# A decoder trunk on one core: x blocks on ScalarE's queue, a first weight copy on VectorE, nine warming products

## Chip, cores and metric

The kernel runs on one core of one Trainium2 chip. Its engines are TensorE (PE; its weight loads are shown apart as PEld), VectorE (DVE), ScalarE (ACT), GpSimd (POOL) and SyncE (SP), which here only issues DMAs. The metric is the device time of one execution in microseconds; less is better.

## The reference, cut to what matters

Four pre-norm residual layers over one sequence of 256 tokens and 1024 features, all in float32. Layers 0 and 3 use differential attention, layer 1 block attention, layer 2 sliding-window attention with sinks; each is followed by a squared-ReLU MLP.

```python
h = x                                    # (1, 256, 1024)
for i in range(4):
    a = rms_norm(h, attn_norm_g[i])
    h = h + mixer_i(a)                   # qkv = a @ w_in; rotary; softmax; @ v; @ w_out
    h = h + sqrelu_mlp(rms_norm(h, mlp_norm_g[i]), mlp_w_up[i], mlp_w_down[i])
return rms_norm(h, final_norm_g)

def diff_attention(...):                 # layer 0, where the change lies
    q, k, v = split(h @ w_in)            # 1024 x 3072
    q, k = rope(q) / 8, rope(k)          # first quarter of each head's 64 features
    p = softmax(q1 k1) - lam * softmax(q2 k2)   # causal, per head
    o = rms_norm(p @ v, sub_g) * (1 - lambda_init)
    return o @ w_out
```

## The kernel before

The residual stream is held transposed: features on the 128 partitions, tokens along the columns, in four tiles hT (two blocks of 128 features x 256 tokens each). Weights stream from memory in pieces of 128 x 2048 float32 (1 MB), numbered in order of use; `fetch` issues the DMA of a piece into a tile `raw` (four buffers), always on SP's queue.

A product of two float32 matrices is made of three faster ones. `stage` splits each weight piece into a high part `whi`, rounded to the format that TensorE reads at full speed (ScalarE, L176), and a low part `wlo`, the rest (VectorE, L177). `norm_part` splits a block of the normed input in the same way into the two parts of `hg` (ScalarE L330, VectorE L331), with the gain of the norm folded in. Products are hg-high x whi, hg-low x whi and hg-high x wlo. whi and wlo have three buffers each (LOOK + 1), so the high part of a piece can be written only when TensorE has read that of three pieces before for the last time. The factor of the norm is found beside the products and applied when they leave PSUM: `norm_sum` squares hT on ScalarE (`sq`, L335) and adds up on VectorE (`acc`, L340 and L344); the products `p_sum` with a matrix of ones sum over the partitions, and GpSimd makes the factor `nr`.

The first two pieces are the start of the kernel. They come in quarters of 256 KB, each followed on SP's queue by one of the eight blocks of x (128 KB), and `stage` works on them quarter by quarter, each with its block. `proj` with `ahead` takes a step of six products (`p_in`) for each block of 128 features as soon as both have come. The next two pieces come in halves. Before the first real product TensorE multiplies a tile of ones by itself WARM = 12 times (`p_warm`).

Beside that VectorE works out the angles of the rotary embedding (`rotary_tables`, tiles an, an_lo, turns) and ScalarE their sine and cosine (`sn`, `cc`), for which it loads another function table. When the first projection has left PSUM as `qk` (L695), `rope` turns it with ropea and ropeb (L406 to L411), TensorE transposes it (`p_qk`), and the parts go to `qhl` and `kpad` for the scores `p_s`, whose exponentials are transposed (`p_t`) and multiplied by v (`p_av`); the outcome `o` (L509) is transposed again (`p_o`).

The order on each engine is set by a scheduler when the program is built; the engines then run in that order and wait for semaphores. DMAs use eight semaphores in turn, so a ninth transfer is issued only when the first has landed. The kernel can add a constraint of order alone: `behind(tc, late, ahead)`. The table TURNS names pairs of TensorE instructions, by layer, tile and number, of which the first is put behind the second.

Of the kernel before, what the change touches and what calls it, by code (L numbers as in the profile page):

```python
# [14 lines left out]
AF = mybir.ActivationFunctionType  # L15
OP = mybir.AluOpType
# [4 lines left out]
S = 256  # L21
# [6 lines left out]
NEG = -1.0e38  # L28
LOOK = 2
FAR = 5  # L30
WARM = 12
RAW = 4


# [17 lines left out]
        (("p_s", 4), ("p_in", 116)),  # L52
        (("p_s", 42), ("p_d", 38)),
        (("p_d", 150), ("p_d", 161)),
    ),
    1: (
        (("p_sum", 0), ("p_in", 31)),
# [45 lines left out]
def f(ap):  # L103
    return ap.bitcast(F32)
# [24 lines left out]
def behind(tc, late, ahead):  # L129

    tc.add_manual_dep(late, ahead.name, mybir.DependencyInfo(mybir.DependencyClass.NoSync, mybir.DependencyReason.DATA),
                      reason="behind")
# [3 lines left out]
def trunk(ctx: ExitStack, tc: tile.TileContext, xT, gains, lams, swa_row, fng, weights, out):  # L136
    nc = tc.nc
    V, A, G, T = nc.vector, nc.scalar, nc.gpsimd, Numbered(nc.tensor)
# [6 lines left out]
    def bank(tag, name):  # L145
        return ps.tile([P, 512], F32, tag=tag, name=name, bufs=4)

    def room(j, shape, name, dt=F32):

        return sb.tile(shape, dt, tag=f"slot{j}", name=name, bufs=1)  # L150
# [4 lines left out]
    def fetch(parts=1, along=None):  # L155

        i = len(fetched)
        raw = sb.tile([P, 2048], F32, tag="raw", name=f"raw{i}", bufs=RAW)
        w = 2048 // parts
        for h in range(parts):  # L160
            s = slice(h * w, (h + 1) * w)
            nc.sync.dma_start(raw[:, s], weights[i, :, s])
            if along:
                along()
        fetched.append(raw)

    def stage(w=1024, first=None):
        i = len(staged)
        raw = fetched[i]
        hi = sb.tile([P, 2048], F32R, tag="whi", name=f"whi{i}", bufs=LOOK + 1)  # L170
        lo = sb.tile([P, 2048], F32R, tag="wlo", name=f"wlo{i}", bufs=LOOK + 1)
        for h in range(2048 // w):
            if first:
                first()
            s = slice(h * w, (h + 1) * w)
            high = A.activation(hi[:, s], raw[:, s], AF.Copy)  # L176
            V.tensor_tensor(lo[:, s], raw[:, s], f(hi[:, s]), op=OP.subtract)  # L177
        highs.append(high.ins)
        staged.append((hi, lo))

    used = [0]

    def take():
        i = used[0]
        used[0] += 1
        while len(fetched) < min(weights.shape[0], i + FAR + 1):
            fetch()
        while len(staged) < min(weights.shape[0], i + LOOK + 1):
            stage()
        return staged[i]  # L190
# [5 lines left out]
    hT = [cst.tile([P, 512], F32, name=f"hT{j}") for j in range(4)]  # L196
    xv = xT.rearrange("(b p) t -> p b t", p=P)
    gn = cst.tile([P, 2 * DEPTH * 8 + 2 + NT], F32, name="gn")
    gv = gn[:, :2 * DEPTH * 8].rearrange("p (k l b) -> p k l b", k=2, l=DEPTH)
    sg = gn[:, 2 * DEPTH * 8:2 * DEPTH * 8 + 2]  # L200
    posi = gn[:, 2 * DEPTH * 8 + 2:].bitcast(I32)
    loaded = []

    def load_x():
        d = len(loaded)
        nc.sync.dma_start(hT[d // 2][:, S * (d % 2):S * (d % 2) + S], xv[:, d, :])
        loaded.append(d)

    first_act = cst.tile([P, 1], F32, name="first_act")
    V.memset(first_act, 0.0)  # L210
    A.activation(first_act, first_act, AF.Copy)
    nc.sync.dma_start(gn, gains)
    fetch(4, load_x)
    fetch(4, load_x)
    fetch(2)
    fetch(2)

# [12 lines left out]
    warm = bank("wk", "p_warm")  # L230
    for _ in range(WARM):
        T.matmul(warm[:, :P], ones, ones, start=True, stop=True)
# [10 lines left out]
    def bcast(dram, n):  # L243
        return bass.AP(tensor=dram.tensor, offset=dram.offset, ap=[[0, P], [1, n]])
# [6 lines left out]
    def rotary_tables():  # L251

        posf = cst.tile([P, NT], F32, name="posf")
        V.tensor_copy(posf, posi)
        an = cst.tile([P, NT, 8], F32, name="an")
        lo = cst.tile([P, NT, 8], F32, name="an_lo")
        V.tensor_tensor(an, invt, posf[:, :, None].to_broadcast([P, NT, 8]), op=OP.mult)
        G.memset(lo, 0.0)

        for turn, bits in ((2.0 ** 16 * math.pi, 10), (2.0 * math.pi, 9), (2.0 * math.pi, 20)):  # L260
            q = cst.tile([P, NT, 8], F32, name="turns")
            V.tensor_scalar(q, an, 1.0 / turn, None, op0=OP.mult)
            V.tensor_scalar(q, q, 12582912.0, None, op0=OP.add)
            V.tensor_scalar(q, q, -12582912.0, None, op0=OP.add)
            for x in (an, an, lo):
                m, e = math.frexp(turn)
                c = math.ldexp(math.floor(m * 2 ** bits), e - bits)
                turn -= c
                V.scalar_tensor_tensor(x, q, -c, x, op0=OP.mult, op1=OP.add)
            if bits == 10:  # L270
                yield
            V.scalar_tensor_tensor(lo, q, -turn, lo, op0=OP.mult, op1=OP.add)
            if bits != 20:
                V.tensor_tensor(q, an, lo, op=OP.add)
                V.tensor_tensor(an, an, q, op=OP.subtract)
                V.tensor_tensor(lo, an, lo, op=OP.add)
                V.tensor_copy(an, q)
        V.tensor_tensor(an, an, lo, op=OP.add)
        pi = 3.1415925
        V.tensor_scalar(an, an, pi, -pi, op0=OP.min, op1=OP.max)  # L280
        ab = cst.tile([P, NT, 8], F32, name="ab")
        V.scalar_tensor_tensor(ab, an, -1.0, an, op0=OP.mult, op1=OP.max)
        V.tensor_scalar(ab, ab, -1.0, math.pi / 2, op0=OP.mult, op1=OP.add)
        A.activation(sn, an, AF.Sin)
        A.activation(cc[:, :, 0:8], ab, AF.Sin)
        V.tensor_copy(cc[:, :, 8:16], cc[:, :, 0:8])
        V.tensor_scalar(nsn, sn, -1.0, None, op0=OP.mult)

    def lambdas():
        lam_init = [0.8 - 0.6 * math.exp(-0.3 * i) for i in (0, 3)]  # L290
        lv = room(4, [P, 4, 2, HD], "lv")
        nc.sync.dma_start(lv, bcast(lams, 8 * HD))
        lp = sb.tile([P, 2, 2, HD], F32, tag="ropea", name="lp")
        V.tensor_tensor(lp, lv[:, 0::2], lv[:, 1::2], op=OP.mult)
        ls = cst.tile([P, 2, 2], F32, name="ls")
        V.tensor_reduce(ls, lp, axis=AX.X, op=OP.add)
        A.activation(ls, ls, AF.Exp)
        V.tensor_tensor(nlam, ls[:, 1], ls[:, 0], op=OP.subtract)
        for s in range(2):
            V.tensor_scalar(nlam[:, s:s + 1], nlam[:, s:s + 1], -lam_init[s], None, op0=OP.add)  # L300
            V.tensor_scalar(sg[:, s:s + 1], sg[:, s:s + 1], 1.0 - lam_init[s], None, op0=OP.mult)

    def rsqrt(y, x, n, by_power=False):

# [19 lines left out]
    def norm_part(n, d):  # L324

        j, b = d // 2, d % 2
        if b == 0:
            n.both.append(sb.tile([P, 2, 2, S], F32R, tag=f"hg{j}", name=f"hg{j}", bufs=1))
        both, h, g = n.both[j][:, b], hT[j][:, S * b:S * b + S], n.gain[:, d:d + 1]
        A.activation(both[:, 0], h, AF.Copy, scale=g)  # L330
        V.scalar_tensor_tensor(both[:, 1], h, g, f(both[:, 0]), op0=OP.mult, op1=OP.subtract)  # L331

    def norm_sum(n, j):
        sq = sb.tile([P, 512], F32, tag="relu", name="sq")
# [251 lines left out]
    def mixer_layer(i, n):  # L586
# [46 lines left out]
        else:  # L633
# [36 lines left out]
            def LAM(_):  # L670
                if i == 0:
                    lambdas()
# [53 lines left out]
    def into(n, d, p, row, whole=False):  # L726

        j, b = d // 2, d % 2
        h = hT[j][:, S * b:S * b + S]
        y = p  # L730
        if not whole:
            y = sb.tile([P, S], F32, tag="y", name="y")
            joined(y, p)
        if row is not None:
            V.tensor_tensor(y, y, row, op=OP.mult)
        V.tensor_tensor(h, y, h, op=OP.add)  # L736
        norm_part(n, d)
        if b:
            norm_sum(n, j)
# [78 lines left out]
    def down_out(us, res, factor):  # L818
# [35 lines left out]
        for c in range(2):  # L854
# [29 lines left out]
            else:  # L884
# [10 lines left out]
                finish(1, 2)  # L895

    tables = rotary_tables()
    next(tables)
    n = new_norm(gv[:, 0, 0, :])
    blocks = iter(range(8))  # L900
    for _ in range(2):
        stage(512, lambda: norm_part(n, next(blocks)))
# [114 lines left out]
```

## Time and profile before

| | |
|---|---|
| Median of 3 runs | 1141.01 us (1140.76 to 1141.21) |
| Profiled execution | 1140.76 us; its span is 1139.0 us |
| TensorE busy | 1130.0 us, 99% of the span |
| VectorE, ScalarE busy | 825.5 us (72%), 660.7 us (58%) |
| Read from memory | 196.52 MB, 173 GB/s over the span |
| Mean granted clock of TensorE | 0.999 |

The span goes from the first instruction of the program to the last; the time of an execution has a little more around it. A row of the timeline has start and duration in us, engine (a q behind it stands for the queue that issues DMAs), line, operation, output and inputs by the program's names, sizes, a count where equal rows were merged, and in brackets how long the engine had been idle and what released it. A name without its number stands for all buffers of that name.

### The profile page before, as it was taken

How to read it: one execution, taken by the hardware profiler on the slowest of the kernel's cores; microseconds unless marked ns; L12 is line 12 of the kernel's file. 1: busy time of each engine (PE TensorE's matmuls, PEld its weight loads, DVE VectorE, ACT ScalarE, POOL GpSimd, SP SyncE). 2: the span in 40 equal slices, each digit the busy share in tenths (PEclk: the TensorE clock that was granted, in tenths of full speed). 3: DMA queues.
4: the chain of work that ended last, by engine and by line, in shares of the span. 5: the costliest groups of instructions: out<-in, count | busy, mean ns of one | idle time of the engine just before them, and what ended most of it. 6: DMA issues, size and time to landing. Idle time of an engine off the chain costs nothing.

```text
span 1139.0 us, 17026 instructions
## 1 busy us (share of the span) xinstructions
PE 1130.0 (99%) x6560; PEld 986.0 (87%) x6560; DVE 825.5 (72%) x1584; ACT 660.7 (58%) x1207; POOL 13.2 (1%) x43
## 2 busy tenths in 40 slices
PE   9999999999999999999999999999999999999997
PEld 8889988888888888888899998888888899888886
DVE  8878977656676698766569887765667788777453
ACT  7866656544476665654446765554446766665342
POOL 2000000000000000000000000000000000000000
PEclk9999999999999999999999999999999999999999
DMA  8543555555544355555553346555554435554551
GB/s 330 197 148 118 175 197 196 196 193 185 185 148 148 116 181 190 197 201 189 185 209 112 111 152 218 185 187 191 190 200 138 145 134 164 197 195 167 185 185 37
DMA packets 30608, 198.66 MB, mean 174 GB/s; under 512 B 3520, under 2 KB 5184, under 8 KB 7360
## 3 DMA queue, kind: packets, MB, share of 16 engines
q1 hardware_dynamic: 30240, 197.06, 50.2%
q8 instruction: 51, 0.84, 0.3%
q10 hardware_dynamic: 288, 0.52, 0.1%
q14 instruction: 29, 0.24, 0.1%
HBM read 196.52 MB, written 1.05 MB: 173 GB/s over the span
## 4 chain that ended last, share of the span: by engine, by line
PE 94%; DVE 3%; issue 1%; ACT 1%; DMA 0%; SPq 0%; POOLq 0%; POOL 0%; DVEq 0%; ACTq 0%
PE p_up L118 31%; PE p_down L118 23%; PE p_in L118 17%; PE p_last L118 7%; PE p_d L118 6%; PE p_s L118 3%; PE p_av L118 2%; PE p_t L121 1%; DVE wlo L177 1%; PE p_qk L121 1%; PE p_e L118 1%; DMA raw<-in_weights 0%; PE p_o L121 0%; ACT junk L504 0%; ACT whi L176 0%
## 5 line engine op out<-in xcount | busy, mean ns | idle before, releaser
L177 DVE TENSOR_TENSOR wlo<-raw,whi 128x1024 fp32r<-128x1024 f32 (+1 forms) x374 | 446.5, 1209 | 201.3 <-ACT whi L176 200.8
L176 ACT ACTIVATE whi<-raw 128x1024 fp32r<-128x1024 f32 (+1 forms) x374 | 383.8, 1046 | 207.8 <-issue 110.5
L118 PE MATMUL p_up<-hg,whi 128*128 128x512 f32 x1024 | 356.1, 394 | 0.0
L118 PE MATMUL p_up<-hg,wlo 128*128 128x256 f32 x1024 | 283.7, 278 | 0.0
L118 PE MATMUL p_down<-uu,whi 128*128 128x512 f32 x768 | 266.4, 393 | 0.0
L118 PEld LDWEIGHTS p_up<-hg,whi 128*128 128x128 f32 x1024 | 191.7, 187 | 43.4
L118 PE MATMUL p_down<-uu,wlo 128*128 128x256 f32 x768 | 213.5, 278 | 0.0
L118 PE MATMUL p_in<-whi,hg 128*128 128x512 f32 (+1 forms) x736 | 212.7, 371 | 0.0
L118 PEld LDWEIGHTS p_up<-hg,wlo 128*128 128x128 f32 x1024 | 192.6, 188 | 0.5
L118 PEld LDWEIGHTS p_down<-uu,whi 128*128 128x128 f32 x768 | 143.9, 187 | 32.8
L118 PEld LDWEIGHTS p_in<-whi,hg 128*128 128x128 f32 x736 | 132.9, 189 | 22.4 <-ACT hg L330 0.2
L118 PEld LDWEIGHTS p_down<-uu,wlo 128*128 128x128 f32 x768 | 144.5, 188 | 0.0
L118 PE MATMUL p_in<-wlo,hg 128*128 128x512 f32 (+1 forms) x368 | 130.1, 368 | 0.0
L118 PE MATMUL p_d<-oo,whi 128*128 128x256 f32 (+1 forms) x416 | 85.0, 295 | 0.0
L803 ACT ACTIVATE uu<-u 128x512 fp32r<-128x512 f32 x64 | 40.5, 632 | 73.4 <-DVE u L801 73.4
L118 PE MATMUL p_last<-whi,uu 128*128 128x512 f32 (+1 forms) x264 | 79.4, 383 | 0.0
L118 PEld LDWEIGHTS p_in<-wlo,hg 128*128 128x128 f32 x368 | 68.8, 189 | 11.4 <-DVE wlo L177 0.5
L723 ACT ACTIVATE cross<-p_up 128x256 f32<-128x256 f32 x128 | 47.9, 374 | 37.3 <-PE p_up L118 35.3
L118 PEld LDWEIGHTS p_d<-oo,whi 128*128 128x128 f32 x416 | 66.3, 191 | 1.9 <-issue 0.2
L330 ACT ACTIVATE hg<-hT,gn 128x256 fp32r<-128x256 f32 x64 | 31.4, 503 | 60.6 <-DVE hT L736 60.6
L441 ACT ACTIVATE e<-ns,nm 128x256 f32<-128x256 f32 (+1 forms) x128 | 56.8, 446 | 13.5 <-DVE nm L438 13.3
L118 PE MATMUL p_d<-oo,wlo 128*128 128x256 f32 x224 | 63.9, 286 | 0.0
(168 smaller groups left out, 1073.4 us busy)
## 6 DMA issues: line engine op xcount, KB each, us to landing
raw<-in_weights SPq DMA_DIRECT2D x181, 1024.0 KB, 4.8
raw<-in_weights SPq DMA_DIRECT2D x8, 256.0 KB, 4.6
raw<-in_weights SPq DMA_DIRECT2D x4, 512.0 KB, 7.0
hT<-in_xT SPq DMA_DIRECT2D x8, 128.0 KB, 4.5
bias<-in_swa_row SPq DMA_DIRECT2D x1, 512.0 KB, 3.7
grow<-in_fng SPq DMA_DIRECT2D x1, 512.0 KB, 3.5
out<-res SPq DMA_DIRECT2D x4, 128.0 KB, 2.1
out<-res ACTq DMA_DIRECT2D x2, 256.0 KB, 2.2
```

The source lines that it names most:

```text
L118: return self.keep(out.tensor.name.rstrip("_0123456789"), self.engine.matmul(out, *args, **kw))
L121: return self.keep(out.tensor.name.rstrip("_0123456789"), self.engine.transpose(out, *args, **kw))
L176: high = A.activation(hi[:, s], raw[:, s], AF.Copy)
L177: V.tensor_tensor(lo[:, s], raw[:, s], f(hi[:, s]), op=OP.subtract)
L330: A.activation(both[:, 0], h, AF.Copy, scale=g)
L441: A.activation(e[:, s], ns[:, s], AF.Exp, bias=nm[:, t:t + 1], scale=-1.0, accum_out=l[:, t:t + 1])
L723: A.activation(cross, p[:, S:], AF.Copy)
L803: A.activation(both[:, :, 0], r3(2)(u), AF.Copy)
```

## The change

- Four blocks of x (0 to 3) are issued on ScalarE's queue: two ahead of its first table load and two behind `first_act`. SP issues the gains, four quarters of the first weight piece in a row, then block 4, then the second piece's four quarters with blocks 5 to 7 behind the first three.
- The high part of the first quarter of the first piece is copied by VectorE and not by ScalarE. Three constraints put that copy behind an instruction of the angles, the first low part of hg behind the copy, and the first wlo behind that.
- The two scalings of `sg` in `lambdas` are put behind the last instruction of the angles' list.
- WARM is 9 instead of 12.
- Layer 0 has twenty more pairs in TURNS.

In the order that is built from it, TensorE's instructions differ from the old order only within layer 0. There p_sum stands behind the product p_in 56, a little later than before; p_qk is preceded by seven products more of the third projection's start and the second's end; on ScalarE the load of the table for sine stands behind the first half of the sixth weight piece's whi; on VectorE the halves of the third and fourth piece's wlo follow each other with few instructions of the angles between them.

```diff
-WARM = 12
+WARM = 9
 TURNS = {
     0: (
...
+        (("p_sum", 0), ("p_in", 56)),
+        (("p_in", 98), ("p_qk", 7)),
+        (("p_in", 114), ("p_s", 6)),
+        (("p_s", 7), ("p_in", 114)),
+        (("p_in", 115), ("p_s", 11)),
+        (("p_in", 116), ("p_s", 2)),
+        (("p_in", 117), ("p_s", 5)),
+        (("p_t", 0), ("p_in", 136)),
+        (("p_qk", 8), ("p_t", 0)),
+        (("p_t", 1), ("p_qk", 9)),
+        (("p_qk", 10), ("p_t", 2)),
+        (("p_in", 137), ("p_qk", 15)),
+        (("p_s", 12), ("p_in", 158)),
+        (("p_t", 3), ("p_s", 15)),
+        (("p_in", 159), ("p_t", 5)),
+        (("p_s", 13), ("p_in", 161)),
+        (("p_in", 162), ("p_s", 17)),
+        (("p_in", 165), ("p_s", 23)),
+        (("p_t", 6), ("p_in", 173)),
+        (("p_in", 174), ("p_t", 6)),
...
             nc.sync.dma_start(raw[:, s], weights[i, :, s])
             if along:
-                along()
+                along(h)
...
         for h in range(2048 // w):
-            if first:
-                first()
+            normed = first() if first else None
             s = slice(h * w, (h + 1) * w)
-            high = A.activation(hi[:, s], raw[:, s], AF.Copy)
-            V.tensor_tensor(lo[:, s], raw[:, s], f(hi[:, s]), op=OP.subtract)
+            if i + h:
+                high = A.activation(hi[:, s], raw[:, s], AF.Copy)
+                V.tensor_tensor(lo[:, s], raw[:, s], f(hi[:, s]), op=OP.subtract)
+            else:
+                copied = V.tensor_copy(hi[:, s], raw[:, s]).ins
+                behind(tc, copied, angles[1])
+                behind(tc, normed, copied)
+                behind(tc, V.tensor_tensor(lo[:, s], raw[:, s], f(hi[:, s]), op=OP.subtract).ins, normed)
...
-    used = [0]
+    used, angles = [0], []
...
-    def load_x():
+    def load_x(queue=nc.sync):
         d = len(loaded)
-        nc.sync.dma_start(hT[d // 2][:, S * (d % 2):S * (d % 2) + S], xv[:, d, :])
+        queue.dma_start(hT[d // 2][:, S * (d % 2):S * (d % 2) + S], xv[:, d, :])
         loaded.append(d)
 
     first_act = cst.tile([P, 1], F32, name="first_act")
     V.memset(first_act, 0.0)
+    load_x(nc.scalar)
+    load_x(nc.scalar)
     A.activation(first_act, first_act, AF.Copy)
     nc.sync.dma_start(gn, gains)
-    fetch(4, load_x)
-    fetch(4, load_x)
+    load_x(nc.scalar)
+    load_x(nc.scalar)
+    fetch(4)
+    load_x()
+    fetch(4, lambda h: h < 3 and load_x())
     fetch(2)
     fetch(2)
...
-                V.scalar_tensor_tensor(x, q, -c, x, op0=OP.mult, op1=OP.add)
+                angles.append(V.scalar_tensor_tensor(x, q, -c, x, op0=OP.mult, op1=OP.add).ins)
...
-            V.tensor_scalar(sg[:, s:s + 1], sg[:, s:s + 1], 1.0 - lam_init[s], None, op0=OP.mult)
+            late = V.tensor_scalar(sg[:, s:s + 1], sg[:, s:s + 1], 1.0 - lam_init[s], None, op0=OP.mult)
+            behind(tc, late.ins, angles[-1])
...
-        V.scalar_tensor_tensor(both[:, 1], h, g, f(both[:, 0]), op0=OP.mult, op1=OP.subtract)
+        return V.scalar_tensor_tensor(both[:, 1], h, g, f(both[:, 0]), op0=OP.mult, op1=OP.subtract).ins
```

## The prediction

> **What bounds the kernel now.** I read the page first: its busy shares and the chain that ended last.
>
> ```profile
> span 1139.0 us, 17026 instructions
> PE 1130.0 (99%) x6560; PEld 986.0 (87%) x6560; DVE 825.5 (72%) x1584; ACT 660.7 (58%) x1207; POOL 13.2 (1%) x43
> PE 94%; DVE 3%; issue 1%; ACT 1%; DMA 0%; SPq 0%; POOLq 0%; POOL 0%; DVEq 0%; ACTq 0%
> ```
>
> TensorE is busy for 1130.0 of 1139.0 us, and 94% of the chain is its own. The diff touches the first 30 us, and the built order of the changed program differs from the old one in layer 0 alone, so nothing can be won beyond the waits of TensorE there. The windows of the early stretch come next (columns: stretch, its length, busy time of TensorE, weight loads, VectorE, ScalarE, GpSimd, then granted clock, DMA share, GB/s).
>
> ```profile
> 1.00:6.00 5.00, 5.00 (x23) 5.00 (x24) 2.32 (x11) 2.43 (x5) 4.72 (x22) 1.00 0.66 197
> 16.00:30.00 14.00, 13.97 (x66) 11.33 (x65) 13.45 (x43) 11.90 (x15) 0.71 (x1) 1.00 0.92 367
> ```
>
> Two things to see. From 16 to 30 us VectorE is busy for 13.45 of 14.00 us: what is inserted or moved there is late for somebody. And TensorE counts as busy from 1 us on, although until 6 us it only multiplies ones. The timeline shows what ends that, and at which rate the first real products run.
>
> ```profile
> 0.72 1.28 ACT L211 ACT_TABLE_LOAD   x1 [0.72 <-PEq L1006]
> 0.98 5.49 PE L118 MATMUL p_warm<-ones 128*128 128x128 f32 x24 [0.98 <-POOL ones L221]
> 1.17 0.42 SPq L162 DMA_DIRECT2D raw<-in_weights  x1
> 1.64 0.42 SPq L206 DMA_DIRECT2D hT<-in_xT  x1
> 4.68 0.63 ACT L176 ACTIVATE whi<-raw 128x512 fp32r<-128x512 f32 x1 [2.46 <-DMA raw<-in_weights]
> 5.22 0.49 ACT L330 ACTIVATE hg<-hT,gn 128x256 fp32r<-128x256 f32 x1
> 5.35 0.69 DVE L177 TENSOR_TENSOR wlo<-raw,whi 128x512 fp32r<-128x512 f32 x1 [0.93 <-ACT whi L176]
> 6.12 1.48 PE L118 MATMUL p_in<-whi,hg 128*128 128x512 f32 x4
> 7.90 1.09 PE L118 MATMUL p_in<-whi,hg 128*128 128x512 f32 x4
> 8.80 0.33 SPq L162 DMA_DIRECT2D raw<-in_weights  x1
> 9.29 1.08 PE L118 MATMUL p_in<-whi,hg 128*128 128x512 f32 x4
> 18.53 0.17 DVE L277 COPY an<-turns 128x16 f32<-128x16 f32 x1
> ```
>
> The operands of the first product, whi and hg, are ready at 5.22 + 0.49 = 5.71 us, but the twelve warming products last to 6.12 (0.43 us each, from 5.14 / 12). The first step of six products takes 7.90 - 6.12 = 1.78 us, the second 9.29 - 7.90 = 1.39. The excess of 0.39 us is that of 1.7 products which take 0.46 instead of 0.23 us: TensorE runs at half its rate until about 6.9 us, whatever the clock column says.
>
> **The change, part by part.** Landings first (KB, us from issue to landing, for the first weight quarter, the first block of x and the last quarter of the second piece):
>
> ```profile
> raw<-in_weights SPq DMA_DIRECT2D x1, 256.0 KB, 3.5
> hT<-in_xT SPq DMA_DIRECT2D x1, 128.0 KB, 3.4
> raw<-in_weights SPq DMA_DIRECT2D x1, 256.0 KB, 4.5
> ```
>
> *Queues.* The quarter lands at 1.17 + 3.5 = 4.67 us, the block behind it at 1.64 + 3.4 = 5.04, so 128 KB more cost 0.37 us. In the changed program SP issues the quarter at the same place, and ScalarE's queue brings two blocks of x beside it. The quarter then lands between 4.67 (nothing shared) and 5.04 (one block ahead of it); I take 4.9. The four issues cost ScalarE some 0.4 us each and push its table load and first_act back by 0.8 us; its fourth issue waits for the landing of block 0, with the first hg behind it in the queue. ScalarE has 2.46 us of idle time before its first whi to hide all that. If the cover were gone, hg would be late and the first product with it, by up to the 1.6 us of the four issues. The bytes in all are the same, so I leave the landing of the last quarter (issued at 8.80, landing at 13.3) where it is.
>
> *Copy on VectorE.* The trace has no copy of 512 columns there. It costs at least 0.17 us (16 columns) and at most 0.69 (wlo, same size, two sources); I take 0.5, nearer to the row of its size. First product: 4.9 + 0.5 = 5.4 us, between 4.9 and 5.8.
>
> *Nine warming products.* They end at 0.98 + 9 x 0.43 + 0.2 = 5.0 us, so they no longer hold the first product, and TensorE stands idle for some 0.4 us. The 0.7 us between 5.4 and 6.12 are run at half rate, so the head start is worth 0.36 us (0.15 to 0.6). In the row TensorE was busy without a break from 0.98 us and the rate doubled at 6.9. [...]
>
> *First low part of the third weights.* The rows of before, from the last quarter on:
>
> ```profile
> 13.55 0.62 ACT L176 ACTIVATE whi<-raw 128x512 fp32r<-128x512 f32 x1
> 14.47 0.62 ACT L335 ACTIVATE sq<-hT 128x512 f32<-128x512 f32 x1
> 14.76 0.69 DVE L177 TENSOR_TENSOR wlo<-raw,whi 128x512 fp32r<-128x512 f32 x1
> 15.36 0.48 DVE L331 SCALAR_TENSOR_TENSOR hg<-hT,gn,hg 128x256 fp32r<-128x256 f32 x1
> 15.76 0.68 DVE L340 TENSOR_TENSOR acc<-acc,sq 128x512 f32<-128x512 f32 x1
> 16.48 0.42 DVE L344 TENSOR_TENSOR acc<-acc 128x256 f32<-128x256 f32 x1
> 17.26 0.60 PE L118 MATMUL p_sum<-ones,acc 128*128 128x128 f32 x4
> 17.32 1.22 DVE L177 TENSOR_TENSOR wlo<-raw,whi 128x1024 fp32r<-128x1024 f32 x1
> 18.60 0.19 PEld L118 LDWEIGHTS p_in<-wlo,hg 128*128 128x128 f32 x1 [0.47 <-DVE wlo L177]
> ```
>
> Before, wlo of the last quarter ends at 15.45, and 1.87 us later (hg, one acc, the folding acc, four small ones) VectorE starts the first half of the third piece's wlo; TensorE waits for it at 18.60. In the changed order ScalarE does a square (0.62) ahead of the last quarter's whi, so that whi ends at about 13.3 + 0.6 + 0.6 = 14.5 and its wlo at 15.3, and between it and the next wlo stand two acc instead of one (+0.6), no hg (-0.4), and three small ones (-0.1): 2.0 us. The wlo starts at 17.3 and TensorE goes on at about 18.5, as before; the head start is lost in this wait, which grows. By then TensorE had also done the two products p_sum, which a new pair of TURNS puts eleven products later; they are worth about 4 x 0.11 = 0.45 us and are still to be done. So TensorE is 0.45 - 0.1 = 0.35 us behind here. If the last quarter's chain comes 0.8 us earlier, it is 0.45 ahead; if it comes 0.3 later, 0.65 behind.
>
> *Rotary tables and p_qk.*
>
> ```profile
> 23.23 1.28 ACT L284 ACT_TABLE_LOAD   x1
> 25.37 0.22 ACT L284 ACTIVATE sn<-an 128x16 f32<-128x16 f32 x1 [0.86 <-DVE an L280]
> 26.45 0.20 ACT L285 ACTIVATE cc<-ab 128x16 f32<-128x16 f32 x1
> 27.12 2.00 ACT L176 ACTIVATE whi<-raw 128x1024 fp32r<-128x1024 f32 x2
> 27.73 1.22 DVE L177 TENSOR_TENSOR wlo<-raw,whi 128x1024 fp32r<-128x1024 f32 x1
> 28.87 0.42 DVE L411 TENSOR_TENSOR qk<-ropea,ropeb 128x256 f32<-128x256 f32 x1
> 29.60 1.03 PE L121 MATMUL p_qk<-ident,qk 128*128 128x128 f32 x8
> 76.50 5.46 PE p_in L118 x24
> ```
>
> Before, ScalarE loads its Sin table at 23.23, ahead of the two halves of the sixth piece's whi (27.12). In the changed order the first of these halves stands ahead of the table load, and it waits until TensorE has read the third piece's whi for the last time, since three buffers take turns. Counted from the end of that read: half a whi 1.05, table 1.28, sn 0.22, cc 0.20, less 0.1 for each overlap, is 2.5 us; the second half of the whi ends at 3.5; on VectorE its wlo (1.22) now stands between the rotary products and the sum qk, so 4.7; qk (0.42) ends at 5.1, and p_qk can start at about 5.2. TensorE has 21 products between that read and p_qk in the changed order, 22 distances of 0.2275 us (5.46 / 24) less the 0.4 us that the read itself lasts: 4.6 us. So it waits 0.6 us, and 0.1 more for a weight load that is no longer hidden: +0.7 us (0 if the table is loaded ahead after all, 1.2 if VectorE is half a us late as well). Before, TensorE met qk without an idle row. Queued behind the waiting whi on ScalarE are the tables, the other half and the next qk; all of layer 0 waits for p_qk.
>
> *Later in layer 0.*
>
> ```profile
> 35.16 0.35 PE L118 MATMUL p_s<-kpadl,qhl 128*128 128x256 f32 x1 [0.15 <-DVE kpadl L584]
> 65.70 0.69 DVE L509 TENSOR_TENSOR o<-p_av,ry 128x512 f32<-128x512 f32 x1
> 66.94 0.60 PE L121 MATMUL p_o<-ident,o 128*128 128x128 f32 x4
> ```
>
> From p_qk to the first p_s there are as many products as before, so the small wait at 35.16 stays. Between the first p_av and p_o there are three fewer: 0.68 us of cover against 66.94 - 66.39 = 0.55 of slack, +0.1 us (0 to 0.5). The two scalings of the gains (0.4 us in all) only move, into a VectorE that is waited for; they are in the terms above.
>
> Sum: +0.35 + 0.7 + 0.1 = +1.15 us on the profiled execution (1140.76 us, its span and 1.76 around it): 1141.9. The median of the three runs is 1141.01, 0.25 above the profiled one, so I forecast a median of 1142.1 us. What a measurement of this kernel can tell from no change is about 0.2%, or 2.3 us: edges at 1138.7 and 1143.3. My forecast is a loss too small to tell.
>
> **The rivals.** *The half rate lasts longer.* [...] A quarter: 0.25.
>
> *The waits don't come and the head start stays.* VectorE and ScalarE had 0.9 and 2.5 us of idle time before their first work; if x comes early enough that both are 0.8 us ahead at the last quarter, the first term is -0.45, and if the sixth piece's whi does not hold the table, the second is 0: 1140.6 on the median's scale, and 1140.0 with the small waits gone as well. Against it speaks the order in the built program. 0.18. To be faster by over 0.2% it would also need the waits that stand in the rest of the layer to go, perhaps a third of this.
>
> *The streaming is late.* SP has at most eight transfers under way; the second piece's quarters wait for landings of the first ones, and these now share with x. If the last quarter lands 1 us later, the first low part is 1 us later: 1143.1. The row of 4.5 us for a quarter under load against 3.5 at the start speaks for it, the equal bytes against it. 0.07.
>
> **How the numbers follow.** Forecast 0.5, rivals 0.25, 0.18 and 0.07. Slower by over 0.2%: 0.18 of the first rival, 0.05 of the third, 0.05 from a forecast whose terms all end at their upper bounds (0.65 + 1.2 + 0.5 = 2.35): 0.28. Faster by over 0.2%: 0.06. Within: 0.66. The range goes from 1140.0 (second rival) to 1143.9 (first rival with half a us more), which leaves out no more than 2 in 10.
>
> **What would show it.** Right: the first p_in at about 5.4 us after a gap, the first p_in from the third piece's wlo still at 18.3 to 18.8, an idle row before p_qk of about 0.6 us with ScalarE's Sin table loaded behind a half of whi, less than 5 us ahead of p_qk. The half-rate rival shows in a second and third step of 2.7 us instead of 1.39. Wrong: no idle row at p_qk, or the low part before 17.8 us; then the second rival holds. A wait anywhere else in layer 0 over 0.5 us that I have not named would make the sum wrong even at the right time.

## The result and the profile after

The changed kernel took 1143.64 us (median of 12 runs, 1142.57 to 1144.59), the kernel before 1140.95 (12 runs, 1140.46 to 1141.74). The ratio is 1.0023, 95% interval 1.0016 to 1.0031: 2.7 us slower, 0.24%. The profiled execution of the changed kernel took 1144.19 us, 3.43 more than that of the kernel before (1140.76).

From the page of the changed kernel, busy times and the chain that ended last:

```profile
span 1142.4 us, 17013 instructions
PE 1129.5 (99%) x6554; PEld 982.6 (86%) x6554; DVE 826.2 (72%) x1585; ACT 660.1 (58%) x1206; POOL 13.2 (1%) x43
PE 96%; DMA 1%; DVE 1%; issue 1%; ACT 1%; SPq 0%; POOLq 0%; POOL 0%; DVEq 0%; ACTq 0%
```

TensorE does the same work but for the three warming products, the span is 3.4 us longer, and a DMA has 1% of the chain, where it had 0%. The windows of the early stretch (length, then busy time of TensorE, weight loads, VectorE, ScalarE, GpSimd, granted clock, DMA share, GB/s):

```profile
1.00:6.00 5.00, 4.03 (x18) 3.84 (x18) 1.93 (x8) 2.33 (x4) 4.72 (x22) 1.00 0.76 210
16.00:30.00 14.00, 12.03 (x53) 9.08 (x52) 12.40 (x35) 10.33 (x13) 0.71 (x1) 1.00 0.95 377
```

From 16 to 30 us TensorE is busy for 12.03 instead of 13.97 us, and VectorE and ScalarE, which were to be the cause of any loss, have more idle time than before. All of them wait for something from outside. The timeline shows the start, and then what is waited for:

```profile
0.98 4.05 PE L138 MATMUL p_warm<-ones 128*128 128x128 f32 x18 [0.98 <-POOL ones L252]
5.48 0.81 DVE L200 CAST whi<-raw 128x512 fp32r<-128x512 f32 x1 [1.06 <-DMA raw<-in_weights]
6.43 1.16 PE L138 MATMUL p_in<-whi,hg 128*128 128x512 f32 x4 [1.40 <-DVE whi L200]
7.98 1.21 PE L138 MATMUL p_in<-whi,hg 128*128 128x512 f32 x4
16.34 0.63 ACT L196 ACTIVATE whi<-raw 128x512 fp32r<-128x512 f32 x1 [1.94 <-DMA raw<-in_weights]
16.88 1.14 ACT L367 ACTIVATE sq<-hT 128x512 f32<-128x512 f32 x2
17.00 0.69 DVE L197 TENSOR_TENSOR wlo<-raw,whi 128x512 fp32r<-128x512 f32 x1 [1.80 <-ACT whi L196]
17.70 0.69 DVE L372 TENSOR_TENSOR acc<-acc,sq 128x512 f32<-128x512 f32 x1
18.49 0.69 DVE L372 TENSOR_TENSOR acc<-acc,sq 128x512 f32<-128x512 f32 x1
19.21 0.43 DVE L376 TENSOR_TENSOR acc<-acc 128x256 f32<-128x256 f32 x1
20.83 0.50 PE L138 MATMUL p_in<-wlo,hg 128*128 128x512 f32 x1 [0.95 <-DVE wlo L197]
22.78 0.60 PE L138 MATMUL p_sum<-ones,acc 128*128 128x128 f32 x4
```

The first product is later than before (6.43 against 6.12), not earlier. ScalarE then stands idle for 1.94 us until the last quarter of the second piece has landed; VectorE idles behind it, and the first product on the third piece's low part starts at 20.83 instead of 18.60. That is 2.23 of the 3.43 us. The landings (KB, us from issue to landing) of the first weight quarter, issued at 1.17, and of the last quarter of the second piece, issued at 9.29:

```profile
raw<-in_weights SPq DMA_DIRECT2D x1, 256.0 KB, 4.3
raw<-in_weights SPq DMA_DIRECT2D x1, 256.0 KB, 7.0
```

They land at 5.45 and 16.32; before, at 4.66 and 13.26. The last quarter is also issued later, at 9.29 and not at 8.80. SP's rows in the timeline show where the queue stands still:

```profile
3.07 0.43 SPq L232 DMA_DIRECT2D hT<-in_xT  x1
5.66 0.33 SPq L182 DMA_DIRECT2D raw<-in_weights  x1
9.29 0.43 SPq L182 DMA_DIRECT2D raw<-in_weights  x1
```

SP issues nothing from 3.50 to 5.66 us. The wait ends 0.02 us after block 1 of x, which ScalarE's queue had issued at 1.18, has landed (5.64). The row waits for the semaphore of that block: the 212 transfers of the trace have eight between them, and the blocks on ScalarE's queue take some of these.

The rest of the loss, 1.20 us, comes behind the low part, and p_qk carries most of it:

```profile
29.33 1.07 ACT L196 ACTIVATE whi<-raw 128x1024 fp32r<-128x1024 f32 x1 [0.36 <-PE p_in L138]
30.41 1.28 ACT L315 ACT_TABLE_LOAD   x1
31.93 1.05 ACT L196 ACTIVATE whi<-raw 128x1024 fp32r<-128x1024 f32 x1
33.01 1.23 DVE L197 TENSOR_TENSOR wlo<-raw,whi 128x1024 fp32r<-128x1024 f32 x1
34.16 0.42 DVE L443 TENSOR_TENSOR qk<-ropea,ropeb 128x256 f32<-128x256 f32 x1
34.72 1.06 PE L141 MATMUL p_qk<-ident,qk 128*128 128x128 f32 x8 [0.67 <-DVE qk L443]
70.32 0.42 PEld L141 LDWEIGHTS p_o<-ident,o 128*128 128x128 f32 x4 [0.30 <-ACT v L722]
```

A half of whi waits for TensorE, the Sin table stands behind it, a wlo stands ahead of qk, and TensorE waits for qk. The distance from the start of the product ahead of it to its own is 0.83 us longer than such a distance without a wait. p_o has a wait of its own (0.26 us by the same count), the first p_s of layer 0, which waited 0.33 us before, has none.

### The profile page after: what moved, and what is told of

Same layout as the page of the kernel before. It is cut to its first block, busy times and chain, and to the rows that moved or that the text cites. A ratio compares the mean times of both kernels' runs of the same rounds, so it can differ in the third digit from the quotient of the medians.

```text
span 1142.4 us, 17013 instructions
## 1 busy us (share of the span) xinstructions
PE 1129.5 (99%) x6554; PEld 982.6 (86%) x6554; DVE 826.2 (72%) x1585; ACT 660.1 (58%) x1206; POOL 13.2 (1%) x43
## 3 DMA queue, kind: packets, MB, share of 16 engines
q10 hardware_dynamic: 864, 1.05, 0.3%
HBM read 196.52 MB, written 1.05 MB: 173 GB/s over the span
## 4 chain that ended last, share of the span: by engine, by line
PE 96%; DMA 1%; DVE 1%; issue 1%; ACT 1%; SPq 0%; POOLq 0%; POOL 0%; DVEq 0%; ACTq 0%
PE p_up L138 31%; PE p_down L138 23%; PE p_in L138 18%; PE p_last L138 7%; PE p_d L138 6%; PE p_s L138 3%; PE p_av L138 2%; PE p_t L141 1%; DMA raw<-in_weights 1%; PE p_qk L141 1%; PE p_e L138 1%; DVE wlo L197 0%; PE p_o L141 0%; ACT junk L536 0%; PE p_sum L138 0%
## 5 line engine op out<-in xcount | busy, mean ns | idle before, releaser
L473 ACT ACTIVATE e<-ns,nm 128x256 f32<-128x256 f32 (+1 forms) x128 | 56.8, 446 | 13.1 <-DVE nm L470 12.9
```

The source lines that it names most:

```text
L473: A.activation(e[:, s], ns[:, s], AF.Exp, bias=nm[:, t:t + 1], scale=-1.0, accum_out=l[:, t:t + 1])
```

## The experiments

**What is held.** The order of the instructions is made by a scheduler that looks at the loads too, so a change of the loads alone would change the order as well. In all kernels below but r_same the order of computation on TensorE, VectorE and ScalarE is therefore held, by a chain of dependences that adds no semaphore, to that of the kernel before ("old order") or of the changed one ("new order"):

```diff
+    for engine, places in ORDER.items():
+        for late, ahead in zip(places[1:], places):
+            behind(tc, made[engine][late], made[engine][ahead])
```

The table has them all. Landing is that of the last quarter of the second piece: the trace has sixteen events for each transfer (3392 for 212 in the kernel before), read here as one from each of the core's sixteen DMA engines; the columns give the eighth and the last of them. "Low part" is the start of the first product on the third piece's low part. The profiled time and the low part stand with their difference to the kernel before, "rest" is the one difference less the other. Times in us.

| kernel | loads, order | landing: 8th, last | low part | profiled | rest | median (runs) |
|---|---|---|---|---|---|---|
| before | old, old | 12.32, 13.26 | 18.60 | 1140.76 | | 1140.96 (33) |
| changed | new, new | 13.21, 16.32 | 20.83 (+2.23) | 1144.19 (+3.43) | 1.20 | 1143.64 (12) |
| r_same | new, new | 13.86, 16.22 | 20.74 (+2.14) | 1144.09 (+3.33) | 1.19 | 1143.87 (6) |
| p_old_loads | old, new | 12.90, 13.54 | 20.00 (+1.40) | 1143.35 (+2.59) | 1.19 | 1142.92 (10) |
| p_new_loads | new, old | 13.08, 15.84 | 20.38 (+1.78) | 1142.49 (+1.73) | -0.05 | 1142.72 (11) |
| p_old_order | new, old | 13.38, 16.01 | 20.55 (+1.95) | 1142.78 (+2.02) | 0.07 | 1142.68 (11) |
| p_x_between | see there, new | 12.40, 12.98 | 18.96 (+0.36) | 1142.29 (+1.53) | 1.17 | 1142.85 (11) |
| p_quarters | see there, new | 13.46, 15.62 | 20.13 (+1.53) | 1143.25 (+2.49) | 0.96 | 1142.62 (11) |
| p_spacer | see there, new | 13.72, 14.75 | 19.71 (+1.11) | 1143.01 (+2.25) | 1.14 | 1142.59 (11) |
| p_tables | new, see there | 13.37, 15.84 | 20.35 (+1.75) | 1143.40 (+2.64) | 0.89 | 1143.40 (11) |
| p_swap | see there, old | 12.66, 14.58 | 19.11 (+0.51) | 1141.18 (+0.42) | -0.09 | 1141.18 (11) |
| p_copy_only | old, old | 12.67, 13.51 | 18.82 (+0.22) | 1140.98 (+0.22) | 0.00 | 1140.98 (11) |
| p_xb_old | see there, old | 12.35, 14.17 | 19.77 (+1.17) | 1141.81 (+1.05) | -0.12 | 1141.62 (11) |
| p_tuned | old, see there | 12.53, 13.21 | 19.11 (+0.51) | 1141.32 (+0.56) | 0.05 | 1141.12 (11) |

The column "rest" is the main finding: whatever the loads, the profiled time is that of the kernel before, plus the delay of the low part, plus nothing in the old order and 1.1 to 1.2 us in the new one (0.96 in p_quarters). From the first product of layer 0's MLP (`p_up`) to the end, all fourteen profiled executions take 1019.4 to 1019.8 us, so the differences arise ahead of it. The kernel before ran beside each series, with medians of 1140.95 to 1141.08. The intervals of the ratios are about 0.0009 to either side, 1 us, so the medians alone separate only the larger steps.

**r_same: was the late landing chance?**

> The changed kernel once more, unaltered, for a second profile. Theory A (the new loads make the last quarter of the second piece land late each time): it lands at 16.0 to 16.6 us again, two DMA engines behind the other fourteen by over 2 us, the first product on the third piece's low part starts at 20.5 to 21 us, and the median is 1143.6. Theory C (two DMA engines were late by chance in the one execution that was profiled): it lands by 14.5 us, the low part is taken up by 19.3 us, and the profiled execution takes 1142.8 us or less.

```profile
16.25 0.63 ACT L196 ACTIVATE whi<-raw 128x512 fp32r<-128x512 f32 x1 [1.14 <-DMA raw<-in_weights]
20.74 0.50 PE L138 MATMUL p_in<-wlo,hg 128*128 128x512 f32 x1 [1.09 <-DVE wlo L197]
```

The timeline of the second profile repeats the first: landing at 16.22, low part at 20.74, median 1143.87 (ratio 1.0027, 1.0015 to 1.0038). Theory C falls. One engine lagged this time, by 1.3 us, not two.

**Loads and order, crossed: p_old_loads, p_new_loads, p_old_order.** The first is the changed kernel with

```diff
-    load_x(nc.scalar)
-    load_x(nc.scalar)
     A.activation(first_act, first_act, AF.Copy)
     nc.sync.dma_start(gn, gains)
-    load_x(nc.scalar)
-    load_x(nc.scalar)
-    fetch(4)
-    load_x()
-    fetch(4, lambda h: h < 3 and load_x())
+    fetch(4, lambda h: load_x())
+    fetch(4, lambda h: load_x())
```

the second the kernel before with the reverse of it, the third the changed kernel, loads and all, in the old order.

> The changed kernel with the loads of the kernel before (quarters and blocks of x alternate on SP's queue), every engine's order of computation held to that of the changed kernel. Theory A (loads): the last quarter lands at 13.3 us as in the kernel before, the first product on the third piece's low part starts at 18.5 to 19.0, only the wait for p_qk (0.7 us) and what was predicted for p_sum (0.35) and p_o (0.1) remain, and the median is 1142.0 (1141.7 to 1142.4). Theory B (the new order of the engines costs it all): 1143.6 (1143.2 to 1144.0), as with the new loads.

> The kernel before with the new loads alone (four blocks of x on ScalarE's queue, the first four quarters in a row on SP's), every engine's order of computation held to that of the kernel before, twelve warming products, ScalarE making the first high part. Theory A (loads): the last quarter lands at 16 us, the first product on the third piece's low part at 20.5 instead of 18.6, the median is 1143.0 (1142.4 to 1143.6). Theory B (order): 1141.0 (1140.6 to 1141.4), whatever the landings do.

> The changed kernel (new loads, the copy on VectorE, nine warming products) with every engine's order of computation held to that of the kernel before: p_sum early, the Sin table ahead of the sixth piece's high part; the scalings of the gains stay late. Theory A (loads): within 0.3 us of the kernel before with the new loads alone, 1143.0, since a head start is lost in the wait for the low part. Theory B (order): 1141.0 or, with a head start of 0.4 us kept, 1140.6.

p_new_loads came out at 1142.72 us (ratio 1.0017, 1.0008 to 1.0026), p_old_order at 1142.68 (1.0015, 1.0006 to 1.0024): theory A, and the copy with nine warming products is worth nothing beside it. In the timeline of p_new_loads the last quarter's high part waits for its landing as in the changed kernel:

```profile
15.86 0.63 ACT L221 ACTIVATE whi<-raw 128x512 fp32r<-128x512 f32 x1 [1.60 <-DMA raw<-in_weights]
20.38 0.50 PE L221 MATMUL p_in<-wlo,hg 128*128 128x512 f32 x1 [0.24 <-DVE wlo L221]
```

p_old_loads missed both theories: 1142.92 (1.0022, 1.0013 to 1.0032). The landing was in time (13.54), the low part was not (20.00). Its timeline says why:

```profile
14.67 0.62 ACT L240 ACTIVATE sq<-hT 128x512 f32<-128x512 f32 x1
15.19 0.61 ACT L240 ACTIVATE whi<-raw 128x512 fp32r<-128x512 f32 x1
15.48 0.68 DVE L240 TENSOR_TENSOR acc<-sq 128x512 f32<-128x512 f32 x1
16.08 0.69 DVE L240 TENSOR_TENSOR wlo<-raw,whi 128x512 fp32r<-128x512 f32 x1
18.72 2.35 DVE L240 TENSOR_TENSOR wlo<-raw,whi 128x1024 fp32r<-128x1024 f32 x2
20.00 0.50 PE L240 MATMUL p_in<-wlo,hg 128*128 128x512 f32 x1 [0.91 <-DVE wlo L240]
```

In the new order a square stands ahead of the last quarter's whi on ScalarE, and an acc ahead of its wlo on VectorE. With the old loads ScalarE reaches that whi at 15.19, 1.65 us after the landing and 1.64 later than before (13.55). So both halves of the change delay the same low part by themselves, 1.78 and 1.40 us, and together by 2.23: the delays overlap.

**What delays the last quarter: p_x_between, p_quarters, p_swap, p_spacer.** In the changed kernel a block of x stands ahead of each quarter of the second piece, and the first half of the third piece directly behind the last. The four kernels: in the changed one, blocks behind the quarters again,

```diff
     fetch(4)
-    load_x()
-    fetch(4, lambda h: h < 3 and load_x())
+    fetch(4, lambda h: load_x())
```

the third piece in quarters,

```diff
-    fetch(2)
+    fetch(4)
     fetch(2)
```

a spare block between the last quarter and the third piece,

```diff
     fetch(4, lambda h: h < 3 and load_x())
+    nc.sync.dma_start(room(12, [P, 512], "spare")[:, :S], xv[:, 7, :])
```

and, in the kernel before, the last block and the last quarter exchanged (the number is that of the blocks issued behind each quarter):

```diff
-    fetch(4, load_x)
+    fetch(4, lambda h: (1, 1, 2, 0)[h])
```

> The changed kernel with one thing undone in the loads: in the second piece each block of x stands behind a quarter again (quarter, x, quarter, x ... instead of x, quarter, x, quarter ...), so that the last block, not the first half of the third piece, follows the last quarter on SP's queue. Order of computation as in the changed kernel. Theory A1 (the last quarter is late for the bytes ahead of it): one block of 128 KB less, 0.4 us, landing at 15.6 to 15.9 us, median 1143.4. Theory A2 (it is late because the transfers right behind it, with rows of 4 KB, take the bandwidth from the engines that lag): landing at 13.3 to 14.2, the third piece's low part taken up at 18.9 to 19.3, median 1142.2 (1141.9 to 1142.6).

> The changed kernel with the third piece fetched in four quarters instead of two halves, so that rows of 2 KB instead of 4 KB stand behind the last quarter of the second piece. Order of computation as in the changed kernel. Theory A1 (bytes ahead): the last quarter lands at 16.0 to 16.3 as before, median 1143.6. Theory A2 (large rows behind it): landing at 13.5 to 14.5 us, median 1142.2 to 1142.8.

> The kernel before with two neighbours in SP's queue exchanged: the last block of x is issued ahead of the last weight quarter of the second piece, not behind it, so that the first half of the third piece follows the quarter directly. Nothing else changes, and every engine's order is that of the kernel before. Theory A1 (128 KB more ahead of the quarter is what counts): landing at 13.6 to 13.9 us instead of 13.3, median 1141.1 (1140.9 to 1141.4). Theory A2 (what counts is that the half with its rows of 4 KB stands right behind it): landing at 15.4 to 16.2, the third piece's low part taken up at 20 us, median 1142.4 (1141.8 to 1143.0).

> The changed kernel with one load more: the last block of x is fetched a second time, into a buffer that nobody reads, between the last quarter of the second piece and the first half of the third. Order of computation as in the changed kernel. Theory A1 (bytes ahead): the quarter lands at 16.0 to 16.3 as in the changed kernel and the median is 1143.7 or, for 128 KB more ahead of the third piece, 1144.0. Theory A2 (what follows): landing at 13.4 to 14.2, the third piece's low part taken up at 19 to 19.5, median 1142.8 (1142.3 to 1143.1).

Rows of p_x_between, p_quarters, p_spacer and p_swap, from their timelines in this order:

```profile
14.31 0.61 ACT L240 ACTIVATE whi<-raw 128x512 fp32r<-128x512 f32 x1
18.96 0.51 PE L240 MATMUL p_in<-wlo,hg 128*128 128x512 f32 x1 [0.92 <-DVE wlo L240]
```

```profile
15.64 0.63 ACT L240 ACTIVATE whi<-raw 128x512 fp32r<-128x512 f32 x1 [0.69 <-DMA raw<-in_weights]
20.13 0.51 PE L240 MATMUL p_in<-wlo,hg 128*128 128x512 f32 x1 [0.98 <-DVE wlo L240]
```

```profile
15.04 0.62 ACT L240 ACTIVATE whi<-raw 128x512 fp32r<-128x512 f32 x1
19.71 0.50 PE L240 MATMUL p_in<-wlo,hg 128*128 128x512 f32 x1 [0.92 <-DVE wlo L240]
```

```profile
14.60 0.63 ACT L221 ACTIVATE whi<-raw 128x512 fp32r<-128x512 f32 x1 [1.01 <-DMA raw<-in_weights]
19.11 0.50 PE L221 MATMUL p_in<-wlo,hg 128*128 128x512 f32 x1 [0.23 <-DVE wlo L221]
```

Where a block stands behind the quarter (p_x_between, p_spacer), the row of the last quarter's whi waits for no DMA any more, and what stands ahead of it on ScalarE sets its start; where the third piece follows, the wait is there. Neither theory holds alone; the landings of p_quarters (15.62), p_spacer (14.75) and p_swap (14.58) lie between the two expectations. The landing has two parts. The eighth engine is through at 12.3 to 12.9 us where the last block stands behind the quarter and at 12.7 to 13.9 where it stands ahead (eight kernels, p_swap with 12.66 the lowest): that is A1, some 0.8 us between the means (12.53 and 13.34). All of it is in the issue: the quarter is issued at 8.63 us on average in the first six kernels and at 9.48 in the eight, and from the issue to the eighth engine it takes 3.90 and 3.87 us. So the place in the queue makes the issue later, and the transfer itself is not slower up to the eighth engine. The last engine trails the eighth by 1.9 to 3.1 us in the seven kernels in which the third piece follows the quarter directly, and by 0.6 to 1.8 in the seven in which a block does: that is A2, and it is the larger part. The two groups nearly touch (p_swap 1.92, p_xb_old 1.82) and only the changed kernel was profiled twice, so that the third piece behind the quarter makes the lag is likely and not shown. The size of the rows does not explain it: with rows of 2 KB behind the quarter (p_quarters) the lag was 2.16 us, of the same kind as with 4 KB. What slows the one to four late engines was not found.

In time: p_x_between 1142.85 (1.0016, 1.0007 to 1.0025), p_quarters 1142.62 (1.0012, 1.0003 to 1.0021), p_spacer 1142.59 (1.0014, 1.0005 to 1.0023), each 0.8 to 1.3 us below the changed kernel's two medians, which is at the edge of what medians separate here; in the profiled executions 1.9 us lie between p_x_between and the changed kernel. p_x_between's median is 0.25 us above what A2 allowed; p_quarters' is within A2 although its landing was nearer to A1; p_swap's with 1141.18 (1.0002, 0.9993 to 1.0011) within A1 although its landing was between the two.

**p_tables: the tables ahead again.** Up to p_sum and the first two qk as in the changed kernel, from there on the old order:

> The changed kernel up to p_sum and the first two qk; from there on every engine in the order of the kernel before, so that the Sin table is loaded ahead of the sixth piece's high part and the 17 later turns are undone. Loads new, last quarter at 16.0 to 16.3 us. As predicted for this part: the wait of 0.83 us at p_qk and that of 0.26 at p_o go, that at the first p_s (0.3 us) comes back, median 1142.9 (1142.7 to 1143.1). Rival (what waits at p_qk is late from the landing of the third piece and waits elsewhere): 1143.5 to 1143.9.

```profile
32.08 0.86 PEld L239 LDWEIGHTS p_qk<-ident,qk 128*128 128x128 f32 x8 [0.52 <-issue]
37.83 0.36 PE L239 MATMUL p_s<-kpadl,qhl 128*128 128x256 f32 x1 [0.29 <-DVE kpadl L239]
```

1143.40 (1.002, 1.0011 to 1.0029), between the two expectations. In its timeline the wait at p_qk shrinks from 0.83 to 0.28 us, that at p_o is gone, and that at p_s is back with 0.46 instead of 0.33. Worked out: p_sum behind the low part 0.45, plus 0.28, plus 0.46 - 0.33, is 0.86; the "rest" of the table is 0.89. For the changed kernel the same count is 0.45 + 0.83 + 0.26 - 0.33 - 0.11 (a later p_s that waits 0.11 instead of 0.22) = 1.10, against 1.20.

**p_copy_only: the head start alone.** The kernel before with the copy, nine warming products and the late scalings:

```diff
-WARM = 12
+WARM = 9
-            high = A.activation(hi[:, s], raw[:, s], AF.Copy)
+            copied = V.tensor_copy(hi[:, s], raw[:, s]).ins
...
```

> The kernel before with the copy on VectorE and nine warming products alone (and the scalings of the gains late), old loads, every engine's order held to that of the kernel before. First product at 5.4 to 5.6 us instead of 6.12. Theory D (a head start is lost in the wait for the third piece's low part): 1140.9 (1140.6 to 1141.2). Rival (the head start stays): 1140.4 to 1140.6.

```profile
4.54 0.60 DVE L241 CAST whi<-raw 128x512 fp32r<-128x512 f32 x1
5.50 0.75 PE L241 MATMUL p_in<-whi,hg 128*128 128x512 f32 x2 [0.31 <-ACT hg L241]
18.82 0.19 PEld L241 LDWEIGHTS p_in<-wlo,hg 128*128 128x128 f32 x1 [0.50 <-DVE wlo L241]
```

The first product comes 0.6 us earlier, the low part does not: 1140.98 us (0.9999, 0.999 to 1.0007). Theory D holds.

**p_xb_old and p_tuned: a version that beats both?** The first puts the loads of p_x_between, the copy and nine products into the old order. The second is p_copy_only with three places of VectorE's order changed.

> The loads of p_x_between (four blocks of x on ScalarE's queue, the first four quarters in a row, in the second piece each block behind its quarter), the copy on VectorE and nine warming products, with every engine's order of computation that of the kernel before. If the place of the last quarter is all that the new loads cost: landing at 13.0 us, median 1141.0 (1140.6 to 1141.3), 1.7 us less than with the loads as they were changed. If they cost something of their own (blocks of x or the other quarters late): 1141.8 to 1142.7.

> An attempt to beat both: the kernel before with the copy on VectorE and nine warming products, and three places of VectorE's order changed. The third piece's first low part goes ahead of four small instructions of the rotary tables (0.2 us of wait at 18.6 us go, and 0.3 of the head start stays), the second kpadl ahead of a low part (0.33 us of wait at the first p_s), and o ahead of a low part (0.65 us of wait at p_o, 111 us). If all three waits go: 1139.6 (1139.3 to 1140.2). Rival (each low part that is put back is waited for in its place): 1140.7 to 1141.5.

Neither does: 1141.62 (1.0005, 0.9996 to 1.0014), between its two expectations, and 1141.12 (1.0, 0.9991 to 1.0008), as the rival had it. In p_tuned the waits at p_s and at p_o are gone, but the low parts that were put back are waited for, at 21.39 us for instance. In p_xb_old the last quarter landed at 14.17 us and not at 13.0, although a block stands behind it: one engine lagged by 1.4 us, and the first row below waits for it. Its profile shows something else too, in TensorE's rows:

```profile
14.20 0.63 ACT L241 ACTIVATE whi<-raw 128x512 fp32r<-128x512 f32 x1 [0.41 <-DMA raw<-in_weights]
5.86 2.05 PE L241 MATMUL p_in<-whi,hg 128*128 128x512 f32 x4 [0.67 <-DVE whi L241]
7.71 1.05 PE L241 MATMUL p_in<-wlo,hg 128*128 128x512 f32 x2
8.56 1.82 PE L241 MATMUL p_in<-whi,hg 128*128 128x512 f32 x4
10.21 0.63 PE L241 MATMUL p_in<-wlo,hg 128*128 128x512 f32 x2
```

Two products on the low part take 1.05 us at 7.71 and 0.63 at 10.21: half rate until about 10.2 (the trace's record of full rate begins at 10.15, in the kernel before at 6.78). TensorE then never waits for the third piece's low part, which it reaches at 19.77, and the execution is 1.05 us longer than that of the kernel before. This is what the prediction's first rival names, a half rate that lasts longer, in one of the eleven profiled executions with nine warming products.

## Why the prediction was right, and where not

The time lies in the range (1143.64 in 1140.0 to 1143.9), 1.5 us above the point; the loss is just past the edge of what can be told from no change, and the prediction gave a loss of that size 0.28. That the range holds the time is in part luck: its upper end was there for the half rate, which did not come, and the late landing used that room. By the prediction's own sign, the low part at 18.3 to 18.8 us, the sum was wrong, for it came at 20.83.

*The landing of the last quarter* is the step that failed: "The bytes in all are the same, so I leave the landing of the last quarter (issued at 8.80, landing at 13.3) where it is." It landed at 15.8 to 16.3 us in all five profiles with these loads. The bytes ahead of it are one block more, and the transfer that follows it is another. In the changed kernel's profile the 3.06 us are 0.49 of later issue, 0.40 more from the issue to the eighth engine, and 2.16 more from the eighth engine to the last. The third rival named the place and one mechanism, quarters that wait for the landings of earlier transfers, but took the quarter to be 1 us later and gave it 0.07; the lag of the last engines, the larger part, it did not have.

*The first low part.* The chain behind the landing was right: 2.0 us from the end of the last quarter's wlo to the start of the next were forecast, the rows give 19.56 - (17.00 + 0.69) = 1.87. With the landing in time (p_x_between) the low part starts at 18.96, 0.46 later than the 18.5 of the sum. That the order by itself makes the low part 1.40 us later with the old loads (p_old_loads), where the blocks of x come later, the prediction did not see.

*p_sum, p_qk, p_o.* The three terms of the sum that lie behind the low part are 0.45, 0.7 and 0.1, together 1.25; the table's rest is 1.20. p_qk waits 0.83 (0.7 forecast), by the mechanism described, p_o 0.26 (0.1). The small wait at the first p_s went, where it was to stay.

*The start.* The first quarter landed at 4.6 to 5.5 us with the new loads (4.9 forecast, bounds 4.67 to 5.04). The copy took 0.48 to 0.83 us in eleven executions (0.5; the upper bound 0.69 was too low). The first product came at 5.86 to 6.43 with the new loads, 5.4 at the earliest with the old ones. It made no difference, since the head start ends in the wait for the low part, as forecast.

*The rivals.* Half rate: it lasted longer in p_xb_old, which has the old order, and that execution is 1.05 us longer than the kernel before's; it is not what made the changed kernel slow, since neither of its profiles has it. The 1143.9 at the upper end of the range was the author's estimate for this rival, and no run shows its term; what was measured in its place is p_xb_old's profiled execution, 1141.81. Waits that do not come: refuted by p_qk and the low part.

So the sum 1.15 becomes 0.36 for the low part with the landing in time and 1.2 behind it, 1.5 in the profile of p_x_between, and 1.9 more for the landing, 3.4. The medians put 0.8 to 1.3 on the landing; the timed runs have no record of landings, so how often the engines lag that far in them is open.

## What to carry to other kernels

When loads are rearranged, the landing of each later transfer is a term of the sum: ask when it is issued, what stands ahead of it and what directly behind it in the queue, and look at the last of the sixteen engines (16.32 us here, the eighth 13.21), not at the bytes. An order of instructions is made for its landings, so loads and order have to be tried apart, with the order held. And before a start is made earlier, find the next wait that does not move: here it was 12 us later, and a head start of 0.6 us ended there.

## What the runs showed of the hardware

- Within one transfer of 256 KB the last of the sixteen DMA engines ended up to 3.1 us behind the eighth (16.32 and 13.21), and the lag stayed: in the changed kernel two engines trailed the other fourteen in each of the next five transfers too, by 1.3 to 2.2 us. The record of the landings does not name the engines; that they are the same two is an inference.
- The trace's record of TensorE's full rate began at 4.05 to 7.19 us in thirteen of the fourteen profiled executions and at 10.15 in p_xb_old, though its warming products start at 0.98 in each. The records last 1126.40, 1129.81, 1133.23 or 1136.64 us, lengths that are 3.41 apart. In p_xb_old TensorE stood idle from 5.19 to 5.86, and the four products that start then took 2.05 us; in p_tables it stood idle over the same 0.67 us, the full rate began at 5.91, and the same four took 1.19. Why the one execution had it 4.24 us later than the other, no run shows.
- A gap of 1.40 us before the first product in the changed kernel (5.03 to 6.43), after the full rate had begun at 4.73, did not bring the half rate back: the products behind it run at 0.23 us (from 6.97 to 7.20 and to 7.43), where those at half rate in p_xb_old take 0.46 (four from 5.86 to 7.71).
